# Sixteen of 32 experts ranked by token count on the chip, the last eight in blocks of four

## The chip, the cores and the metric

One core of one Trainium2 chip runs the whole kernel. The metric is the device time of one execution in microseconds (us), from its start to its end; the profile's span is the stretch from the first to the last instruction in it.

## The reference, cut to what matters

One layer of a decoder on 288 new tokens (256 of a prompt, 32 of eight samples), D = 2048, all weights float32: a mixer (convolution beside a gated recurrence, between the projections `w_in` and `w_out`), and then a mixture of 32 experts in 4 groups of 8. Each token takes the best group and in it the two best experts.

```python
def _hier_moe(h, w_rg, b_rg, w_re, b_re, w_gate, w_up, w_down):
    x = h.reshape(B * T, D)
    gprob = jax.nn.softmax((x @ w_rg + b_rg).astype(jnp.float32), axis=-1)
    p_top, g_idx = lax.top_k(gprob, 1)
    elog = (x @ w_re + b_re).astype(jnp.float32).reshape(-1, N_GROUPS, EXPERTS_PER_GROUP)
    elog_sel = jnp.take_along_axis(elog, g_idx[:, :, None], axis=1)[:, 0]
    e_val, e_idx = lax.top_k(elog_sel, TOP_K_IN_GROUP)
    e_w = jax.nn.softmax(e_val, axis=-1) * p_top
    ids = g_idx * EXPERTS_PER_GROUP + e_idx
    combine = jnp.sum(jax.nn.one_hot(ids, N_EXPERTS, dtype=jnp.float32) * e_w[..., None], axis=1)
    hid = jax.nn.silu(jnp.einsum('nd,edf->nef', x, w_gate)) * jnp.einsum('nd,edf->nef', x, w_up)
    hid = hid * combine[..., None].astype(hid.dtype)
    y = jnp.einsum('nef,efd->nd', hid, w_down)
    return y.reshape(B, T, D)
```

`w_gate` and `w_up` are 32 x 2048 x 512, `w_down` is 32 x 512 x 2048: 402.7 MB, which have to be read whatever the routing says. With the inputs of the test the experts 0 to 15 have 43, 35, 10, 39, 42, 6, 41, 36, 9, 28, 8, 14, 4, 22, 9 and 8 tokens, the experts 16 to 31 have 11, 17, 16, 17, 7, 36, 17, 7, 14, 21, 6, 8, 8, 26, 10 and 1.

## The kernel before

The stages follow each other in time: the projections of `w_in` with the mixer (to 450 us), 16 columns of `w_out` (to 577 us; `project`, split into a high and a low part), the routing (to 600 us), the experts (to 1592 us) and the final norm.

The experts go in 16 pairs. A `Pair` has 128 slots, 64 for each of its two experts (`CAP`), and tokens are put into slots by one-hot matmuls: `gather(q)` brings a quarter of the normalised tokens `h2` into `xg`, through the one-hot `P`; `gu(vi, q)` multiplies the slots with a quarter of the gate (vi = 0) or up (vi = 1) weights, the first expert in TensorE's columns 0 to 63 and the second in 64 to 127, so that both run side by side; `hidden` is silu times up, `turn` transposes it, `down(h, g)` multiplies with `w_down`, `out` weights the result, `combine` brings it back to the tokens through `PT`. A step, one (vi, q) or one (h, g), needs one load of 1 MiB (1.0486 MB) for each expert: 12 steps and 24 loads a pair, 384 loads in all. `mm` chains all these matmuls, so that TensorE runs them in the order in which they are written. The next pair's gathers stand between the steps of the pair before (`regular_pairs`).

All loads go through one DMA queue, SP's, in the order of use, into a ring of 14 slots: `xa` (3), `xb` (4), `raw` (3), `hi`, `lo` (2 each); a load waits until TensorE has read what its slot held. Four loads are issued during `w_out` (`load_ahead` at c = 3 to 6).

```python
        w = xslot(not isinstance(e, int)).rearrange("p (k c) -> p k c", c=1024 if which == 2 else 512)
        src = view[e, i] if isinstance(e, int) else view[bass.ds(e, 1), i].rearrange("e p k c -> (e p) k c")
        nc.sync.dma_start(out=w, in_=src)
```

Fifteen pairs run in a row; then 7 loads of the sixteenth are issued (`LASTPRE`), and all engines come to a branch: were there experts with over 64 tokens, pairs for these would run here (`overflow`; with these inputs none does). Then `last_pair` runs alone, with its gathers between its own gate steps.

The routing ends in `key`, the slot number of each token's two choices; it takes the place within an expert (`pr`, a triangular matmul over `mb`), the counts (`pn`) and what an overflow would add. The one-hot of pair 0 is made from `key`. ScalarE makes `h2` for the gathers (six activations), and the recurrence's states of heads 4 to 7 of the samples (`late_state`, eight units of two matmuls with a copy each) fill TensorE meanwhile.

Of the kernel before, what the change touches and what calls it, by code (L numbers as in the profile page):

```python
# [29 lines left out]
XPAIRS = 4  # L30
# [6 lines left out]
XA, XB = 3, 4  # L37
PRE = 3
LASTPRE = 7
# [16 lines left out]
def constants():  # L56
    p = np.arange(128)
    bq = np.zeros((8, 8, 4))
    for b in range(8):
# [15 lines left out]
        "full": np.broadcast_to((np.arange(NE) + 1) * float(CAP), (128, NE)),  # L75
        "xbase": np.broadcast_to(EXB - CAP - np.arange(NE) * float(CAP), (128, NE)),
# [28 lines left out]
def trunk_step(ctx: ExitStack, tc: tile.TileContext, a, o):  # L105
# [22 lines left out]
    rbias = const.tile([TT, 36], F32, name="rbias")  # L128
    lbc = const.tile([128, 8], F32, name="lbc")
# [216 lines left out]
    def router_rows():  # L346
# [6 lines left out]
        V.tensor_mul(wr3, wr3, nffn[:, :, None].to_broadcast([128, KT, 36]))  # L353
        nc.sync.dma_start(out=o["new_conv_sample"][0, :, 0:26].rearrange("b w c -> b (w c)"),
# [129 lines left out]
    def gate(j):  # L484
        finish(f"a{j - GB}")
# [327 lines left out]
    cr = sm.tile(list(CONSTS["cr"].shape), F32, name="cr")  # L813
    nc.sync.dma_start(out=cr, in_=a["cr"])
    onb = sm.tile([TT, TT], BF16, name="onb")
    V.memset(onb, 1.0)
    trib = sm.tile([TT, TT], BF16, name="trib")
    e64 = sm.tile([TT, NE], BF16, name="e64")
# [22 lines left out]
    def wlast(e0, e1, q, cuts):  # L841

        ws = [xslot().rearrange("p (k c) -> p k c", c=512) for _ in range(2)]
        for i in range(cuts):
            ks = slice(i * 4 // cuts, (i + 1) * 4 // cuts)
            for w, e in zip(ws, (e0, e1)):
                nc.sync.dma_start(out=w[:, ks], in_=wlv[e, q, :, ks])
        return ws

    def wload(which, e, q):  # L850
        if isinstance(e, int) and (which, e, q) in ahead:
            return ahead.pop((which, e, q))
        view = (wgv, wuv, wdv[:, q // 2])[which]
        i = q % 2 if which == 2 else q
        w = xslot(not isinstance(e, int)).rearrange("p (k c) -> p k c", c=1024 if which == 2 else 512)
# [22 lines left out]
    def late_state():  # L878
        for hh in range(4):
            st = ls0[hh // 2][:, hh % 2]  # L880
            for u in range(2):
                su = st[:, 4 * u:4 * u + 4]
                pn = bank("z")
                T.matmul(pn, lkm[:, hh], lvx[:, 4 * u:4 * u + 4], start=True, stop=False)
                T.matmul(pn, ident, su, start=False, stop=True)
# [5 lines left out]
    def load_ahead(i, e=0):  # L891
        which, q, u = i // 8, i % 8 // 2, i % 2
        ahead[which, e + u, q] = wload(which, e + u, q)

    for c in range(KT):
# [19 lines left out]
        if c == 6:  # L915
            V.tensor_copy(trib, C("tri")[:TT])
            V.tensor_copy(e64, C("e64")[:TT])
        if PRE <= c < PRE + XA + XB - 3:
            with tc.issue_after(loads[-1]):
                load_ahead(c - PRE)  # L920

# [28 lines left out]
    for t in range(NT):  # L950
        for u in range(2):
            us = slice(u * 1024, u * 1024 + 1024)
# [38 lines left out]
    oh = tv([TT, 2, NT, NE], "oh")  # L991
    for i in range(2):
        V.tensor_scalar(pk[:, i], od, float(i), None, op0=ALU.is_equal)
        V.tensor_mul(oh[:, i].rearrange("p t (g e) -> p t g e", e=8), b4(pk[:, i, :, None, :]),
                     b4(ohg[:, :, :, None]))

    pn, pr = bank("tp"), bank("o")
    for u in range(NT):
        T.matmul(pn[:TT, :NE], onb, mb[:, u], start=u == 0, stop=u == NT - 1)
# [6 lines left out]
    exn = tv([TT, NE, 4], "exn")  # L1006
    V.tensor_tensor(exn, pn[:TT, :NE, None].to_broadcast([TT, NE, 4]),
                    C("thr")[:TT, None, :].to_broadcast([TT, NE, 4]), op=ALU.is_gt)
    ex = sv([TT, 2, NE], "ex")
    V.reduce_sum(ex[:, 0], exn, axis=AX.X)  # L1010
    xs1 = sv([TT, NE + 1], "xs1")
    V.memset(xs1[:, 0:1], 0.0)
    V.tensor_tensor_scan(xs1[:, 1:], C("ones")[:TT], ex[:, 0], 0.0, op0=ALU.mult, op1=ALU.add)
    V.scalar_tensor_tensor(ex[:, 1], xs1[:, :NE], float(CAP), C("xbase")[:TT], op0=ALU.mult, op1=ALU.add)

    place = pr[:TT, 0:96].rearrange("p (t e) -> p t e", e=NE)
    kk = tv([TT, 2, NT, NE], "kk")
    key = sv([TT, 2, NT], "key")
    ov = tv([TT, NT, NE], "ov")
    V.tensor_tensor(ov, place, C("full")[:TT, None, :].to_broadcast([TT, NT, NE]), op=ALU.is_ge)  # L1020
    for i in range(2):
        V.tensor_mul(kk[:, i], oh[:, i], place)
    V.reduce_sum(key, kk, axis=AX.X)
    V.tensor_mul(oh, oh, ov[:, None].to_broadcast([TT, 2, NT, NE]))
    V.tensor_mul(oh.rearrange("p i t e -> p (i t) e"), oh.rearrange("p i t e -> p (i t) e"),
                 ex[:, None, 1].to_broadcast([TT, 2 * NT, NE]))
    kx = tv([TT, 2, NT], "kx")
    V.reduce_sum(kx, oh, axis=AX.X)
    V.tensor_add(key, key, kx)

    rows = sv([128, 4, N], "rows")
    xei = sv([1, 9], "xei", I32)
# [27 lines left out]
    def overflow_ids():  # L1060

        xid = sv([1, 8, NE], "xid")
        V.tensor_tensor(xid, xs1[0:1, None, 1:].to_broadcast([1, 8, NE]),
                        C("iota")[0:1, 0:8, None].to_broadcast([1, 8, NE]), op=ALU.is_le)
        xe = sv([1, 9], "xe")
        V.reduce_sum(xe[:, 0:8], xid, axis=AX.X)
        V.tensor_scalar(xe[:, 0:8], xe[:, 0:8], float(NE - 1), None, op0=ALU.min)
        V.tensor_copy(xe[:, 8:9], xs1[0:1, NE:NE + 1])
        V.tensor_copy(xei, xe)

# [22 lines left out]
    class Pair:  # L1093
        def __init__(self, e0, e1, base, last=False):
            self.e, self.base, self.last = (e0, e1), base, last
            self.pg, self.y = [], {}

        def onehot(self):
            kd = key
            self.P = P = X([TT, NT, 128], "P")  # L1100
            if self.base:
                kd = X([TT, 2, NT], "kd")
                V.tensor_scalar(kd, key, -float(self.base), None, op0=ALU.add)
# [53 lines left out]
        def down(self, h, g):  # L1157
# [3 lines left out]
            ws = [wload(2, e, 2 * h + g) for e in self.e]  # L1161
            for k in range(2):
                f = 2 * g + k
                for c in range(2):
                    for u, w in enumerate(ws):
                        mm(self.py[c][64 * u:64 * u + 64], self.hd[:, f, 64 * u:64 * u + 64],
# [49 lines left out]
    def regular_pairs():  # L1216

        ps = [Pair(2 * i, 2 * i + 1, 128 * i) for i in range(NE // 2 - 1)]
        before, py = None, None
        for n, p in enumerate(ps):  # L1220
            after = ps[n + 1] if n + 1 < len(ps) else None
# [172 lines left out]
```

## Time and profile before

| | us |
|---|---|
| median of 3 runs (1616.8 to 1619.52) | 1619.11 |
| the profiled execution | 1617.82 |
| its span | 1616.0 |
| TensorE busy | 1537.7 |
| VectorE busy | 676.2 |
| ScalarE busy | 455.9 |
| GpSimd busy | 31.8 |

The profiled execution lies 1.8 us over its span and 1.3 us under the median. The engines' busy times overlap. PE is TensorE, DVE is VectorE, ACT is ScalarE, SP issues the loads. A matmul of float32 stands as two instructions in the trace, so a step of a pair (8 matmuls) as x16.

### The profile page before, as it was taken

What the parts mean: (1) busy time and instruction counts of PE and PEld (TensorE: products, weight loads), DVE (VectorE), ACT (ScalarE), POOL (GpSimd) and SP (SyncE); (2) the same over time, 40 slices, a digit from 0 to 9 for tenths busy, and PEclk for the clock granted to TensorE, in tenths of its full rate; (3) what the DMA queues carried; (4) which work ended last, traced back from release to release, by engine and by line L of the source; (5) the groups of instructions that cost most, each with busy time, mean ns of one, the idle gap of its engine ahead of it and who ended that gap; (6) DMA issues with size and microseconds to landing.
All of it is one profiled execution on the core that took longest, in us unless ns stands there. A gap on an engine that the chain in (4) does not pass through costs nothing. (4 is left out here: it accounts for less than half of the span.)

```text
span 1616.0 us, 22366 instructions
## 1 busy us (share of the span) xinstructions
PE 1537.7 (95%) x9146; PEld 967.0 (60%) x9146; DVE 676.2 (42%) x1368; ACT 455.9 (28%) x980; POOL 31.8 (2%) x53
## 2 busy tenths in 40 slices
PE   5999999999979979999999999999999999999895
PEld 3999999999879944553553553453454454453431
DVE  4567787986554441312312412412412412312304
ACT  4477775976834450000000000000000000000003
POOL 1000001000000000000000000000000000000000
PEclk9999999999989989999999999999999999999897
DMA  8645456545496449999999999999999999999872
GB/s 210 174 121 144 136 157 195 150 127 142 112 290 166 154 175 343 401 415 410 423 411 415 419 417 402 425 416 412 422 414 416 422 414 414 421 419 410 360 266 59
DMA packets 228309, 492.78 MB, mean 305 GB/s; under 512 B 13593, under 2 KB 157545, under 8 KB 194936
## 3 DMA queue, kind: packets, MB, share of 16 engines
q1 hardware_dynamic: 225448, 485.09, 80.2%
q0 software_dynamic: 2608, 6.13, 1.1%
q8 instruction: 74, 1.21, 0.3%
q14 instruction: 35, 0.29, 0.0%
q10 hardware_dynamic: 144, 0.07, 0.0%
HBM read 483.92 MB, written 8.18 MB: 305 GB/s over the span
## 5 line engine op out<-in xcount | busy, mean ns | idle before, releaser
L1086 PEld LDWEIGHTS tp<-P,h 96*128 96x128 f32 x1536 | 177.8, 194 | 41.5 <-issue 22.0
L1086 PE MATMUL att<-xb,xg 128*64 128x512 f32 x584 | 199.2, 598 | 0.8 <-DVE xg L1117 0.8
L1086 PE MATMUL tp<-P,h 96*128 96x128 f32 x1536 | 187.3, 281 | 9.7 <-DVE xg L1117 4.8
L195 DVE TENSOR_TENSOR lo<-raw,hi 128x1024 fp32r<-128x1024 f32 x124 | 147.7, 1221 | 50.5 <-ACT hi L194 50.3
L194 ACT CAST hi<-raw 128x1024 fp32r<-128x1024 f32 x124 | 123.8, 1049 | 82.5 <-PE z L199 60.6
L1086 PE MATMUL att<-lo,xg 128*64 128x512 f32 x296 | 133.8, 602 | 0.8 <-issue 0.8
L1086 PE MATMUL att<-xa,xg 128*64 128x512 f32 x448 | 132.3, 595 | 1.6 <-DVE xg L1117 1.6
L1171 ACT ACTIVATE yh<-o,wc 128x512 fp32r<-128x512 f32 x64 | 44.0, 687 | 313.5 <-PE o L1086 281.8
L1147 DVE TENSOR_TENSOR hid<-hid,att 128x512 f32<-128x512 f32 x16 | 11.0, 688 | 285.5 <-PE att L1086 285.5
L1086 PE MATMUL att<-raw,xg 128*64 128x512 f32 x432 | 128.4, 595 | 1.6 <-DVE xg L1117 1.6
L1086 PE MATMUL att<-hi,xg 128*64 128x512 f32 x288 | 128.2, 594 | 0.0
L1182 DVE TENSOR_TENSOR acc<-acc,z 96x512 f32<-96x512 f32 x120 | 76.9, 680 | 116.8 <-PE z L1086 116.6
L198 PE MATMUL z<-hhb,hi 128*128 128x288 f32 x368 | 112.1, 305 | 0.0
L200 PE MATMUL z<-hhb,lo 128*128 128x288 f32 x368 | 110.9, 301 | 0.0
L199 PE MATMUL z<-hla,hi 128*128 128x288 f32 x368 | 110.9, 301 | 0.0
L199 PE MATMUL z<-hlb,hi 128*128 128x288 f32 x368 | 110.6, 301 | 0.0
L1117 DVE TENSOR_TENSOR xg<-tp,npm 128x512 f32<-128x512 f32 x64 | 44.3, 692 | 158.0 <-PE tp L1086 157.9
L198 PE MATMUL z<-hha,hi 128*128 128x288 f32 x368 | 110.2, 299 | 0.0
L200 PE MATMUL z<-hha,lo 128*128 128x288 f32 x368 | 109.8, 298 | 0.0
L1172 DVE SCALAR_TENSOR_TENSOR yl<-o,wc,yh 128x512 fp32r<-128x512 f32 x64 | 47.9, 748 | 140.6 <-ACT yh L1171 138.6
L1155 ACT COPY hd<-tp 128x512 f32<-128x512 f32 x16 | 9.4, 586 | 295.3 <-PE tp L1086 295.3
L1146 ACT ACTIVATE hid<-att 128x512 f32<-128x512 f32 x16 | 9.6, 597 | 290.8 <-PE att L1086 248.5
(417 smaller groups left out, 2779.8 us busy)
## 6 DMA issues: line engine op xcount, KB each, us to landing
raw<-in_w_in_dram SPq DMA_DIRECT2D x48, 1024.0 KB, 5.9
xb<-in_w_exp_gate_dram SPq DMA_DIRECT2D x37, 1024.0 KB, 18.6
xb<-in_w_exp_up_dram SPq DMA_DIRECT2D x36, 1024.0 KB, 12.5
xb<-in_w_exp_down_dram SPq DMA_DIRECT2D x35, 1024.0 KB, 13.5
xa<-in_w_exp_gate_dram SPq DMA_DIRECT2D x30, 1024.0 KB, 17.6
raw<-in_w_exp_gate_dram SPq DMA_DIRECT2D x27, 1024.0 KB, 17.4
xa<-in_w_exp_down_dram SPq DMA_DIRECT2D x27, 1024.0 KB, 13.1
raw<-in_w_exp_down_dram SPq DMA_DIRECT2D x27, 1024.0 KB, 13.4
```

The lines of the kernel that those rows point to most:

```text
L194: S.copy(wh[:, ks], w[:, ks])
L195: V.tensor_sub(wl[:, ks], w[:, ks], wh[:, ks].bitcast(F32))
L198: T.matmul(ps[:, :N], wh[:, k], xh[k], start=i == 0, stop=False)
L199: T.matmul(ps[:, :N], wh[:, k], xl[k], start=False, stop=False)
L200: T.matmul(ps[:, :N], wl[:, k], xh[k], start=False, stop=i == KT - 1)
L1086: i = f(*args, **kw)
L1117: V.tensor_mul(self.xg[:, 4 * q:4 * q + 4], pb, npm[:, 4 * q:4 * q + 4, None].to_broadcast([128, 4, 128]))
L1146: si = S.activation(self.hid, self.pg[0], AF.Silu)
L1147: V.tensor_mul(self.hid, self.hid, self.pg[1])
L1171: S.activation(yh, py, AF.Copy, scale=self.wc[:, 2:3])
L1172: V.scalar_tensor_tensor(yl, py, self.wc[:, 2:3], yh.bitcast(F32), op0=ALU.mult, op1=ALU.subtract)
L1182: V.tensor_add(av, av, ps[t][:TT])
```

## The change

Experts 0 to 15 stay in 8 pairs of 64 slots each. Experts 16 to 31 are ranked on the chip by their token count (`keys`, `ids`; the ranks' expert numbers go to `eid`). Ranks 0 to 7 form four pairs of 64 slots, ranks 8 to 15 two blocks of four experts with 32 slots each; `Block` takes the place of `Pair` and gives `128 // len(e)` slots to an expert. The order is: eight pairs, the first block of four, ten loads of the second (`MIDPRE`), the branch, the second block of four, the four ranked pairs, the last of them with the end (`last_down`). A block of four has the same 12 steps as a pair, with four loads in each. The expert numbers of the ranked blocks come from registers, so that their loads (192 of 384) have addresses that are worked out at run time.

The ring gets 16 slots (`XA` 4, `XB` 5), and six loads are issued during `w_out`. The constants `cr` are loaded at the start of the kernel. `h2` is scaled in another order, first halves first. The first one-hot comes from a short key (`key01`, of `pr` and `mb` alone, since the first pair is always experts 0 and 1). Two heads of `late_state` come ahead of the routing, and the other two behind the first gate step in TensorE's fixed order. `last_down` puts its matmuls in the written order too.

```diff
+NST = 16
+NDP = 4
+NQ = 2
-XA, XB = 3, 4
+XA, XB = 4, 5
-LASTPRE = 7
+MIDPRE = 10
...
+        nc.sync.dma_start(out=cr, in_=a["cr"])
...
-    for t in range(NT):
-        for u in range(2):
-            us = slice(u * 1024, u * 1024 + 1024)
+    for u in range(2):
+        us = slice(u * 1024, u * 1024 + 1024)
+        for t in range(NT):
             S.activation(by_four(h2[t][:, us], 0), by_four(acc[:, t, us], 1), AF.Copy, scale=rs2[:, t:t + 1])
...
+    key01 = sv([TT, NT, 2], "key01")
+    V.tensor_add(key01, nm, place[:, :, 0:2])
...
+        V.scalar_tensor_tensor(nj, cnt[:, NST:], float(NE), iot[:, :m], op0=ALU.mult, op1=ALU.subtract)
+        gt = e2[:, 96:96 + m * m].rearrange("p (e f) -> p e f", f=m)
+        V.tensor_tensor(gt, nj[:, None, :].to_broadcast([TT, m, m]), nj[:, :, None].to_broadcast([TT, m, m]),
+                        op=ALU.is_gt)
+        V.reduce_sum(rk, gt, axis=AX.X)
...
+    class Block:
+
+        def __init__(self, es, base, over=False):
+            self.e, self.base, self.over = tuple(es), base, over
+            self.w = 128 // len(self.e)
...
+        def rows(self, u):
+            return slice(self.w * u, self.w * (u + 1))
...
-            ws = [wload(vi, e, q) for e in self.e]
+            ws = [wload(vi, e, q, self.over) for e in self.e]
             for i in range(4):
                 k = 4 * q + i
                 for u, w in enumerate(ws):
-                    mi = mm(self.pg[vi][64 * u:64 * u + 64], self.xg[:, k, 64 * u:64 * u + 64], w[:, i],
+                    mi = mm(self.pg[vi][self.rows(u)], self.xg[:, k, self.rows(u)], w[:, i],
                             start=k == 0, stop=k == KT - 1)
...
-                        if q == 0:
-                            late_state()
+                        if first and q == 0:
+                            late_state((2, 3), mm)
                         if q < 3:
                             p.gather(q + 1)
-                        if q == 0:
+                        if first and q == 0:
                             with tc.issue_after(pi.ins), tc.issue_after(mi.ins):
+                                k = keys()
                                 weights()
-                                overflow_ids()
+                                ids(*k)
...
-                    T.matmul(py[64 * u:64 * u + 64], p.hd[:, f, 64 * u:64 * u + 64], w[:, f], start=f == 0, stop=f == 3)
+                    mm(py[p.rows(u)], p.hd[:, f, p.rows(u)], w[:, f], start=f == 0, stop=f == 3)
...
+    def static_id(j):
+        return nc.values_load(eid[0:1, j:j + 1], engines=[mybir.EngineType.SP], min_val=NST, max_val=NE - 1,
+                              skip_runtime_bounds_check_because="ranks are a permutation of the later experts")
...
+    def quad(i):
+        return Block([static_id(2 * NDP + 4 * i + u) for u in range(4)], b0 + 128 * i)
...
+    in_a_row(blocks + [Later(lambda: quad(0))], first=True)
+    q1 = quad(1)
...
+    for i in range(MIDPRE):
+        load_ahead(i, q1.e)
     regular = nslot[0]
...
-    last_pair(Pair(NE - 2, NE - 1, 128 * (NE // 2 - 1), last=True))
+    in_a_row([q1] + [Later(lambda i=i: Block([static_id(2 * i + u) for u in range(2)], NST * CAP + 128 * i))
+                     for i in range(NDP)], last=True)
```

On TensorE, at the first gate step of the program, before (`h_6200` to `h_6202` are the `h2` of the three token tiles, `z<-xb` the units of `late_state`, `att<-xa` the gate step):

```order
L1086 MATMUL tp<-P,h_6201 128x128
L1086 MATMUL tp<-P,h_6202 128x128
L884 MATMUL z<-xb 128x512
L885 MATMUL z<-xb,ident 128x512
L1086 MATMUL att<-xa,xg 64x512 x8
L1086 MATMUL tp<-P,h_6200 128x128
L1086 MATMUL tp<-P,h_6201 128x128
```

The same place now (`h_6222` to `h_6224`):

```order
L1062 MATMUL tp<-P,h_6224 128x128
L1062 MATMUL att<-xa,xg 64x512 x8
L1062 MATMUL z<-xb 128x512
L1062 MATMUL z<-xb,ident 128x512
L1062 MATMUL z<-xb 128x512
L1062 MATMUL z<-xb,ident 128x512
L1062 MATMUL z<-xb 128x512
L1062 MATMUL z<-xb,ident 128x512
L1062 MATMUL z<-xb 128x512
L1062 MATMUL z<-xb,ident 128x512
L1062 MATMUL tp<-P,h_6222 128x128
```

One unit of `late_state` stood ahead of the first gate step, and two more ahead of the first gather; now four stand between the first gate step and the second gather, and none ahead of the step.

On VectorE, now, from the short key to the start of the long one (`key_6270` is `key01`; the tiles with a k ahead are those of `keys`):

```order
L1014 TENSOR_TENSOR key_6270<-nm,o 96x6
L1162 TENSOR_TENSOR P<-cr,key_6270 96x384
L1075 COPY khd<-o 96x96
L1077 COPY kPT<-tp 96x32
L1081 TENSOR_SCALAR pk<-od 96x24 x2
```

The end of that stretch, 42 rows behind `P` (`xg` is the product of the first gather, that the first gate step reads; `pt<-ge` stands 14 rows behind `P`, and `ge` comes from ScalarE, behind the six activations of `h2`):

```order
L1123 TENSOR_REDUCE kpj<-khid 96x6
L1040 TENSOR_TENSOR wts<-wts,dd 96x3
L1115 TENSOR_TENSOR kPT<-kPT,cr 96x32
L1113 SCALAR_TENSOR_TENSOR kpj<-cr,kPT 96x32
L1180 TENSOR_TENSOR xg<-tp,npm 128x512
```

Before, `xg` of the first gather stood behind the end of the key, the one-hots of two pairs and the weights; now behind most of `keys`, `weights` and `ids`.

On SP's queue, now, loads of the second block of four, ahead of the branch (`eid` holds the expert numbers, an ISA row works out an address):

```order
L1397 TENSOR_LOAD eid
L867 ISA
L867 DMA xa<-in_w_exp_gate_dram 128x2048
L867 ISA
L867 DMA xb<-in_w_exp_gate_dram 128x2048
L867 ISA
L867 DMA xb<-in_w_exp_gate_dram 128x2048
L867 ISA
L867 DMA lo<-in_w_exp_gate_dram 128x2048
```

The same queue before, in a stretch of the loads of the pairs:

```order
L857 DMA xa<-in_w_exp_gate_dram 128x2048 x2
L857 DMA xa<-in_w_exp_up_dram 128x2048
L857 DMA xb<-in_w_exp_up_dram 128x2048
L857 DMA raw<-in_w_exp_up_dram 128x2048 x3
L857 DMA hi<-in_w_exp_up_dram 128x2048
L857 DMA lo<-in_w_exp_up_dram 128x2048
```

Each load of a ranked expert has an ISA row of its own ahead of it, and each of the 16 ranked experts a TENSOR_LOAD; the loads of experts 0 to 15 have neither.

## Rows read from the trace of the kernel before

**Rows 1.** the page: busy time, share of the span and instructions of TensorE

```profile
PE 1537.7 (95%) x9146; PEld 967.0 (60%) x9146; DVE 676.2 (42%) x1368; ACT 455.9 (28%) x980; POOL 31.8 (2%) x53
```

**Rows 2.** timeline of ScalarE: the silu of pairs one and fifteen (start, duration)

```profile
631.20 0.60 ACT L1146 ACTIVATE hid<-att 128x512 f32<-128x512 f32 x1 [12.12 <-PE att L1086]
...
1478.19 0.60 ACT L1146 ACTIVATE hid<-att 128x512 f32<-128x512 f32 x1 [16.88 <-PE att L1086]
```

**Rows 3.** windows: busy time and count by engine, granted clock, DMA share, GB/s

```profile
586.00:596.00 10.00, 2.69 (x13) 1.65 (x13) 7.15 (x40) 8.77 (x7) 0.90 (x1) 0.50 0.00 2
...
700.00:1000.00 300.00, 298.27 (x1572) 139.92 (x1570) 86.87 (x180) 19.66 (x30) 0.00 (x0) 1.00 1.01 416
```

**Rows 4.** waits of the SP queue from 500 us: total, times, longest

```profile
SPq L857 <- PE att L1086: 364.2, 119, 8.8
...
SPq L857 <- PE o L1086: 310.8, 58, 12.0
```

**Rows 5.** windows, as above: inside the steady state, and around the branch

```profile
1020.00:1030.00 10.00, 10.00 (x58) 4.96 (x56) 3.73 (x10) 1.37 (x2) 0.00 (x0) 1.00 1.01 424
...
1508.00:1512.00 4.00, 4.00 (x20) 1.54 (x16) 1.49 (x4) 0.69 (x1) 0.00 (x0) 1.00 1.02 428
...
1512.00:1516.00 4.00, 3.23 (x14) 1.62 (x12) 4.00 (x8) 0.69 (x1) 0.00 (x0) 1.00 0.90 375
...
1516.00:1520.00 4.00, 0.30 (x2) 0.00 (x0) 2.10 (x8) 0.00 (x0) 0.00 (x0) 1.00 0.38 156
...
1520.00:1524.00 4.00, 2.89 (x14) 2.92 (x15) 2.89 (x12) 0.00 (x0) 0.00 (x0) 0.65 0.31 78
```

**Rows 6.** timeline of TensorE in the second pair: one step

```profile
714.57 3.65 PE L1086 MATMUL o<-xb,hd 128*64 128x512 f32 x16
```

**Rows 7.** timeline of TensorE: eight matmuls with 32 columns each

```profile
399.34 0.69 PE L450 MATMUL tp<-sqc,on 128*32 128x288 f32 x8
...
399.96 0.40 PE L198 MATMUL z<-hhb,hi 128*128 128x288 f32 x1
```

**Rows 8.** timelines of ScalarE and VectorE in the routing

```profile
581.50 12.21 ACT L953 ACTIVATE h<-acc,rs 96x1024 f32<-96x1024 f32 x6 [0.61 <-DVE rs L172]
...
594.80 0.16 DVE L1044 TENSOR_REDUCE pt<-ge 96x3 f32<-96x12 f32 x1 [2.25 <-ACT ge L1038]
```

**Rows 9.** timeline of TensorE at the first gather

```profile
600.42 2.84 PE L1086 MATMUL tp<-P,h 96*128 96x128 f32 x24
...
603.10 1.02 PE L884 MATMUL z<-xb 128*128 128x512 f32 x2
...
604.91 3.65 PE L1086 MATMUL att<-xa,xg 128*64 128x512 f32 x16
...
608.50 0.71 PE L1086 MATMUL tp<-P,h 96*128 96x128 f32 x4
```

**Rows 10.** timelines of the SP queue, and of TensorE behind the branch

```profile
1510.69 0.33 SPq L857 DMA_DIRECT2D lo<-in_w_exp_up_dram  x1
...
1521.74 1.28 SPq L857 DMA_DIRECT2D raw<-in_w_exp_up_dram  x3
...
1521.11 5.38 PE L1086 MATMUL tp<-P,h 96*128 96x128 f32 x24 [4.82 <-DVE P L1106]
```

**Rows 11.** timelines at the end, and two groups of the page

```profile
1570.92 3.65 PE L1276 MATMUL o<-xb,hd 128*64 128x512 f32 x16 [0.73 <-ACT hd L1155]
...
1598.30 0.40 PE L1282 MATMUL att<-yl,PT 128*96 128x512 f32 x1
...
1601.45 0.68 DVE L1284 TENSOR_TENSOR acc<-acc,att 96x512 f32<-96x512 f32 x1
...
L1171 ACT ACTIVATE yh<-o,wc 128x512 fp32r<-128x512 f32 x64 | 44.0, 687 | 313.5 <-PE o L1086 281.8
...
L1172 DVE SCALAR_TENSOR_TENSOR yl<-o,wc,yh 128x512 fp32r<-128x512 f32 x64 | 47.9, 748 | 140.6 <-ACT yh L1171 138.6
```

More of the change, by code (lines that the diff above doesn't have):

```diff
@@ L876, in late_loads, with late_state @@
                      C("hm2")[:, :, None].to_broadcast([128, 4, 128]))
-    def late_state():
-        for hh in range(4):
+    def late_state(heads, mul):
+        for hh in heads:
             st = ls0[hh // 2][:, hh % 2]
@@ L920, in trunk_step @@
                 load_ahead(c - PRE)
+    late_state((0, 1), T.matmul)
     def sv(shape, name, dt=F32):
@@ L990, in trunk_step @@
     V.tensor_mul(mb.rearrange("p t (g e) -> p t g e", e=8), b4(pk[:, 2, :, None, :]), b4(ohg[:, :, :, None]))
[L991 to L999, printed above, removed]
+    nm = tv([TT, NT, 2], "nm")
+    V.tensor_scalar(nm, mb[:, :, 0:2], -float(EXB), float(EXB), op0=ALU.mult, op1=ALU.add)
+    pr, pn = bank("o"), bank("tp")
     for t in range(NT):
@@ L1004, in trunk_step @@
         T.matmul(pr[:TT, t * NE:(t + 1) * NE], trib, mb[:, t], start=False, stop=True)
[L1006 to L1014, printed above, removed]
+    for u in range(NT):
+        T.matmul(pn[:TT, :NE], onb, mb[:, u], start=u == 0, stop=u == NT - 1)
     place = pr[:TT, 0:96].rearrange("p (t e) -> p t e", e=NE)
-    kk = tv([TT, 2, NT, NE], "kk")
+    key01 = sv([TT, NT, 2], "key01")
+    V.tensor_add(key01, nm, place[:, :, 0:2])
     key = sv([TT, 2, NT], "key")
[L1019 to L1029, printed above, removed]
     rows = sv([128, 4, N], "rows")
-    xei = sv([1, 9], "xei", I32)
+    xei = sv([1, 2 * XPAIRS + 1], "xei", I32)
+    eid = sv([1, NE - NST], "eid", I32)
     def weights():
@@ L1214, in pair_alone, with in_a_row @@
             p.combine(c, CT)
-    def regular_pairs():
-        ps = [Pair(2 * i, 2 * i + 1, 128 * i) for i in range(NE // 2 - 1)]
-        before, py = None, None
+    def in_a_row(ps, first=False, last=False):
+        prev, py = None, None
         for n, p in enumerate(ps):
-            after = ps[n + 1] if n + 1 < len(ps) else None
+            end = last and n == len(ps) - 1
+            nxt = ps[n + 1] if n + 1 < len(ps) else None
             if n == 0:
@@ L1235, in regular_pairs @@
                                 weights()
-                                overflow_ids()
-                    if before is not None and vi == 0 and q < 2:
-                        before.out(2 + q, py[q])
-                        before.combine(2 + q, CT)
+                                ids(*k)
+                    if prev is not None and vi == 0 and q < 2:
+                        prev.out(2 + q, py[q])
+                        prev.combine(2 + q, CT)
                 if vi == 0:
-                    if after is not None:
-                        after.onehot()
+                    if nxt is not None:
+                        nxt.onehot()
@@ L1243, in regular_pairs @@
+                    if end:
+                        final_weights()
                     p.slots()
-            p.hidden()
-            if after is not None:
-                after.gather(0)
-                after.gather(1)
+            si = p.hidden()
+            if end:
+                last_down(p, si)
+                return
+            if nxt is not None:
+                nxt.gather(0)
+                nxt.gather(1)
             p.turn()
-            if after is not None:
-                after.gather(2)
@@ L1251, in regular_pairs @@
-            py = pair_down(p, (lambda: after.gather(3)) if after is not None else lambda: None)
-            before = p
+            if nxt is not None:
+                nxt.gather(2)
+            py = pair_down(p, (lambda: nxt.gather(3)) if nxt is not None else lambda: None)
+            prev = p
         for c in (2, 3):
-            before.out(c, py[c - 2])
-            before.combine(c, CT)
-    def last_pair(p):
-        p.onehot()
-        p.gather(0)
-        for vi in range(2):
-            for q in range(4):
-                p.gu(vi, q)
-                if vi == 0 and q < 3:
-                    p.gather(q + 1)
-        final_weights()
-        p.slots()
-        si = p.hidden()
+            prev.out(c, py[c - 2])
@@ L1281, in last_pair @@
                 for i, y in enumerate((yh, yl)):
[L1282 removed]
+                    mm(pz[:TT], p.PT[:, t * TT:(t + 1) * TT], y, start=i == 0, stop=i == 1)
                 av = acc[:, t, c * 512:(c + 1) * 512]
@@ L1341, in trunk_step @@
     regular = nslot[0]
-    nx = nc.values_load(xei[0:1, 8:9], min_val=0, max_val=8,
-                        skip_runtime_bounds_check_because="a sum of at most eight overflow tiles")
+    nx = nc.values_load(xei[0:1, 2 * XPAIRS:2 * XPAIRS + 1], min_val=0, max_val=2 * XPAIRS,
+                        skip_runtime_bounds_check_because="a sum of at most nine overflow tiles")
     def overflow(i):
         with tc.If(nx > 2 * i):
-            ids = [nc.values_load(xei[0:1, 2 * i + u:2 * i + u + 1], engines=[mybir.EngineType.SP],
-                                  min_val=0, max_val=NE - 1,
-                                  skip_runtime_bounds_check_because="clamped to the last expert on the chip")
-                   for u in range(2)]
+            xs = [nc.values_load(xei[0:1, 2 * i + u:2 * i + u + 1], engines=[mybir.EngineType.SP],
+                                 min_val=0, max_val=NE - 1,
+                                 skip_runtime_bounds_check_because="clamped to the last expert on the chip")
+                  for u in range(2)]
```

165 lines of the change are left out of this document (117 added, 48 removed).

## The prediction

> **What bounds the kernel now.** I read the page first, then the windows of the expert stage, the silu of each pair, and last the waits of the load queue. TensorE is busy for 1537.7 of the 1616.0 us of the span [rows 1]. In the expert stage it is busy for 298.27 of 300 us at the full clock (granted 1.00, that is 2.4 GHz), while the DMA engines move 416 GB/s with a share of 1.01 [rows 3]. Both look full, so neither row alone tells which one sets the pace. The silu does: the fifteenth stands 1478.19 - 631.20 = 846.99 us behind the first, that is 14 intervals of 60.50 us [rows 2]. A pair's 24 loads of 1.0486 MB in 60.50 us are 416 GB/s, just what the window shows. Who waits for whom is in the queue's own waits: from 500 us on SP waited 364.2 us in 119 places for a gate or up matmul and 310.8 us in 58 for a down matmul, each time for the slot that the matmul read [rows 4]. So the loads wait for TensorE: **the expert stage is bound by TensorE**, with the stream of loads close behind. How close: where slots are at hand the stream shows 424 GB/s in ten microseconds and 428 in four [rows 5]. I take 425, that is 2.467 us a load and 59.2 us a pair. Making TensorE faster by a half would therefore give 2% of the stage and no more; what counts is how far the loads can follow.
>
> **Blocks of four: TensorE.** A step of a pair is 16 instructions in some 3.5 us (3.65 with the last one's tail) [rows 6]: the two experts' columns run side by side. That four column tiles also run together is seen in another stage: eight matmuls with 32 columns each and 288 moving columns are all begun and done in 0.62 us (399.34 to 399.96) [rows 7], where in the step 16 with 512 moving columns take 3.5 us, two by two. By columns, two at a time would want 8/16 x 288/512 x 3.5 = 0.98 us for these eight, four at a time 0.49; the row is nearer to four. So a step of four experts costs TensorE some 3.5 us as a pair's does, and a block of four about 60.5 us, as a pair. Two blocks of four in the place of four pairs take 2 x 60.5 = 121 us of work from TensorE.
>
> **Blocks of four: the stream.** The 384 loads stay. A step of a block of four needs four loads, 9.87 us of the stream; a block needs 48, 118.4 us. There TensorE waits, and the stream sets the pace; in the pairs TensorE sets it again (60.5 against 59.2). So the gain is not 121 us, it is what the loads are ahead: the 1.3 us a pair by which the stream is quicker, and the slots filled when the first block of four begins.
>
> **The front.** The diff makes the way to the first gather shorter, but the order on VectorE puts the product `xg` of that gather behind 42 rows of the long key, and the fourteenth of these, `pt<-ge`, hangs on ScalarE's `ge`, that stands behind six activations of `h2`. Those end at 593.7 and let `pt` start at 594.80 after 2.25 us of waiting [rows 8]; that stays. 28 rows of some 0.2 us follow (`pt` itself took 0.16), so `xg` starts at about 601. The first gate step started at 604.91 before [rows 9], and will at about 601.5. TensorE will have idled since its first gather, and its granted clock was 0.50 (1.2 GHz) in the idle stretch from 586 to 596 [rows 3]; a step that takes 3.6 us at the full clock loses some 3 us at the start. Then four units of `late_state` follow in fixed order, of which one took 604.91 - 603.10 = 1.8 us [rows 9]: 7.2. The second gather starts at 601.5 + 3.6 + 3 + 7.2 = 615.3, before at 608.50 [rows 9]. For the earlier constants `cr` at the start of `w_out` I take 1 us off (0 to 4; nothing shows it directly). The first silu comes at about 631.2 + 6.8 - 1, say **636.6** (632 to 641), so the front loses 5 us.
>
> **The sum.** Seven more static pairs: silu of the eighth at 636.6 + 7 x 60.5 = 1060.1. From a silu to the next pair's first gate step are four up steps and the rest of the pair, 14.0 + 29.4 us (60.5 less 17.1 for four gate steps with two combines between them). The first block of four starts at 1103.5. Of the ring's 16 slots two are then being read and one is in flight: 13 loads of the blocks of four lie there. TensorE waits for the last time at the last up step of the first ranked pair, whose 16th load it needs. Up to it 96 + 16 - 13 = 99 loads have to come, 99 x 2.467 = 244.2 us, and the branch stops the stream once. Before, its windows lost (428 - 375) + (428 - 156) + (428 - 78) GB/s in 4 us each, 2.7 MB or 6.3 us [rows 5], with a next load 11 us behind the last one ahead [rows 10]. Now ten loads lie ahead of it and not seven, and the stop is in the midst of the run; between nothing and 6.3 I take 3.3. That gives 1103.5 + 247.5 = 1351. Then 3.5 for that step, 29.4 for the rest of the pair, 17.1 for the next gate: silu of the second ranked pair at 1401. Two more pairs: 1522.
>
> The end: four up steps 14.0, silu, transposes and `hd` 2.2. Then four times a down step 3.58, the weighting, and a combine. Before, TensorE needed 1570.92 to 1598.70 with adds behind it to 1602.1 [rows 11], since the scheduler put the next down step into the wait. Now the order is as written: TensorE waits each time for 0.69 us on ScalarE and 0.75 on VectorE [rows 11], with hand-overs 1.7, and six combine matmuls take 1.45. 4 x (3.58 + 1.7 + 1.45) = 26.9, but VectorE has no backlog at the end. Last matmul at 1565. From the last add's start to the end of the span are 1616.0 - 1601.45 = 14.6 us [rows 11], which stay: 1580. The profiled execution lies 1.8 over its span, so **1582** (the median shown is another 1.3 higher than that execution; that is in the range).
>
> **Prices that hide.** SP issues a load in 0.33 us, or three in 1.28 [rows 10]; 192 loads now have an address from registers. No row shows such a load. They may cost up to 2.467 us each with nothing lost, since the stream takes that for each. The 42 rows of ranking are in the front already. Weights of the end's norm in the last block, and the six loads ahead during `w_out`, lie beside TensorE's work.
>
> **Where the notes speak against it.** In the last pair before, TensorE idled some 5 us up to 1521.11, and the granted clock was 0.65 in the window behind that; 24 gather instructions took 5.38 us there [rows 10] where they took 2.84 at the full clock [rows 9]. In a block of four TensorE waits 9.87 - 3.5 = 6.4 us in each gate or up step. The Trainium skill, TensorE: Matmul & The Clock Gate, HAM oscillation, says that short bursts with DMA waits between them send the clock back to the lower level at every burst; the rows at the branch agree. At the lower level a step takes 7.1 us, still less than 9.87, so by rule or not the gate and up halves stay with the stream. The skill's page DMA: Bandwidth & Descriptors, Specifications, puts one core's HBM limit at about 358 GB/s; by that 99 loads would take 290 us, not 244, and the time would be 1628. 416 GB/s over 300 us [rows 3] say that it does not hold here.
>
> **Rivals.**
> 1. *The clock stays low in the second half of a block of four too* (downs, gathers, combines). For it: the idle stretches above. Against it: in that half TensorE's work lies closer together, gathers fill the waits. Price: the rest of the second block of four takes 58.8 in the place of 29.4 us behind its loads, and a gate step more: 1582 + 29.4 + 3.5 = 1615, no change. Half of it: 1598. Chance 0.04 for the whole, 0.12 for a part (1587 to 1600).
> 2. *Four tiles run only two by two* with 512 moving columns, 7.1 us a step. Four down steps of the last block lose up to 14 us together, as far as loads don't hide them: 1582 to 1596, middle 1589. Chance 0.05.
> 3. *The stream cannot do more than 416*: 2.521 us a load, 99 x 0.054 = 5.3 more: 1587. Chance 0.12; for it, it is the long run's figure; against it, it is TensorE's pace.
> 4. *The front gets shorter, as the diff's order of the key has it* (`xg` served early in fact, at 594, full clock): silu 8 us sooner, 1574. Chance 0.08.
> 5. *The other side: SP cannot keep up.* Its place is the 192 loads with addresses from registers. At x us each they cost 192 x (x - 2.467); from x = 2.65 on all 36 us are gone, at 3 the time is 1582 + 102 = 1684. For it: each has an instruction of its own ahead of the DMA; against it: 0.33 to 0.43 us for an issue [rows 10]. Chance 0.04.
>
> The forecast itself (1574 to 1590) keeps 0.55. Range 1567 to 1604: it leaves out rival 5, the whole of rival 1, and the edges of 2 and 4. 0.2% (3.2 us) is about what a measurement of this kernel can tell from no change. Faster 0.91, the same 0.04, slower 0.05.
>
> **What the profile after would show.** Silu intervals of 60.5 us for the first eight blocks, near 118 us in the blocks of four, 60.5 again behind them. In the blocks of four SP waits for no slot, GB/s near 425, TensorE half idle, its waits on DMA; a granted clock under 1.00 there, and step durations that tell rivals 1 and 2 apart (starts of four matmuls within 0.03 us, or two). First silu at 632 to 641, `xg` near 601. GB/s under 400 in the blocks of four with SP busy issuing would mean rival 5. The prediction is wrong if the blocks of four take over 125 us each, or if the ranked pairs behind them go on waiting for loads.

## The result and the profile after

The changed kernel takes 1597.94 us (median of 4 runs, 1596.67 to 1599.1), the kernel before 1619.07: a ratio of 0.9872, interval 0.9855 to 0.9889, 21 us faster. Forecast were 1582 and a range of 1567 to 1604. The profiled execution has a span of 1596.6 us, where the sum had 1580.

A line of the page, to compare with [rows 1]:

```profile
PE 1468.3 (92%) x8898; PEld 918.8 (58%) x8898; DVE 644.8 (40%) x1317; ACT 448.2 (28%) x968; POOL 31.9 (2%) x53
```

The silu of some blocks, timeline of ScalarE: the first pair, the two blocks of four, the first, second and fourth ranked pair (as [rows 2]):

```profile
634.09 0.60 ACT L1209 ACTIVATE hid<-att 128x512 f32<-128x512 f32 x1 [12.12 <-PE att L1062]
...
1118.05 0.60 ACT L1209 ACTIVATE hid<-att 128x512 f32<-128x512 f32 x1 [16.91 <-PE att L1062]
...
1247.41 0.60 ACT L1209 ACTIVATE hid<-att 128x512 f32<-128x512 f32 x1 [47.80 <-PE att L1062]
...
1342.49 0.60 ACT L1209 ACTIVATE hid<-att 128x512 f32<-128x512 f32 x1 [17.86 <-PE att L1062]
...
1409.20 0.60 ACT L1209 ACTIVATE hid<-att 128x512 f32<-128x512 f32 x1 [16.88 <-PE att L1062]
...
1530.87 0.60 ACT L1209 ACTIVATE hid<-att 128x512 f32<-128x512 f32 x1 [16.88 <-PE att L1062]
```

The first pairs keep their 60.5 us. From the first to the second block of four 129.4 us pass (branch included), then 95.1 and 66.7, and 60.8 on average behind that. Windows of the same kernel, columns as [rows 3]:

```profile
1101.00:1203.00 102.00, 75.53 (x424) 20.43 (x416) 15.08 (x25) 4.07 (x7) 0.00 (x0) 0.90 1.02 415
1203.00:1224.00 21.00, 10.27 (x49) 6.61 (x52) 8.57 (x36) 0.00 (x0) 0.00 (x0) 0.59 0.76 303
1224.00:1350.00 126.00, 105.94 (x652) 43.27 (x646) 20.82 (x45) 4.53 (x7) 0.00 (x0) 0.95 1.02 416
...
1120.00:1130.00 10.00, 5.75 (x33) 1.32 (x34) 0.00 (x0) 0.00 (x0) 0.00 (x0) 1.00 1.02 423
1160.00:1170.00 10.00, 5.90 (x36) 1.25 (x32) 0.00 (x0) 0.00 (x0) 0.00 (x0) 1.00 1.03 406
1290.00:1300.00 10.00, 7.96 (x64) 2.40 (x66) 0.69 (x1) 0.00 (x0) 0.00 (x0) 1.00 1.02 399
```

In the blocks of four TensorE waits and the stream runs all the time, at 415 to 416 GB/s, but for the branch. The short windows say what that mean is made of: 423 in an up half (the stretch of the four up steps), 406 and 399 in a down half (the four down steps). The up and gate loads bring rows of 8 KB, the down loads rows of 4 KB. And so the prediction's last wait, timeline of TensorE in the up half of the first ranked pair:

```profile
1358.71 3.65 PE L1062 MATMUL att<-hi,xg 128*64 128x512 f32 x14 [1.32 <-DMA hi<-in_w_exp_up_dram]
```

It is the step that was forecast, with the wait for a load that was forecast, 10 us later than its place: 1358.7, where the sum had 1351 less 2.5 for the earlier front.

### The profile page after: what moved, and what is told of

Its sections match the earlier page's. It is cut to its first block, busy times and chain, and to the rows that moved or that the text cites. A ratio compares the mean times of both kernels' runs of the same rounds, so it can differ in the third digit from the quotient of the medians.

```text
span 1596.6 us, 22199 instructions
## 1 busy us (share of the span) xinstructions
PE 1468.3 (92%) x8898; PEld 918.8 (58%) x8898; DVE 644.8 (40%) x1317; ACT 448.2 (28%) x968; POOL 31.9 (2%) x53
## 5 line engine op out<-in xcount | busy, mean ns | idle before, releaser
L1062 PE MATMUL att<-xb,xg 128*64 128x512 f32 (+1 forms) x640 | 175.2, 634 | 11.9 <-DMA xb<-in_w_exp_up_dram 9.6
L1062 PEld LDWEIGHTS tp<-P,h 96*128 96x128 f32 x1344 | 158.3, 196 | 42.8 <-issue 24.0
L1062 PE MATMUL tp<-P,h 96*128 96x128 f32 x1344 | 166.9, 283 | 15.1 <-DVE P L1169 8.6
L1062 PE MATMUL att<-raw,xg 128*64 128x512 f32 (+1 forms) x384 | 119.8, 617 | 8.5 <-DMA raw<-in_w_exp_up_dram 7.0
L1062 PE MATMUL att<-xa,xg 128*64 128x512 f32 (+1 forms) x512 | 106.9, 618 | 10.2 <-DVE xg L1180 6.6
L1245 DVE TENSOR_TENSOR acc<-acc,z 96x512 f32<-96x512 f32 x104 | 66.6, 680 | 118.2 <-PE z L1062 118.0
L1062 PE MATMUL att<-lo,xg 128*64 128x512 f32 (+1 forms) x256 | 101.2, 620 | 2.9 <-DMA lo<-in_w_exp_up_dram 2.9
L1235 DVE SCALAR_TENSOR_TENSOR yl<-o,wc,yh 128x512 fp32r<-128x512 f32 x56 | 41.9, 748 | 150.3 <-ACT yh L1234 148.7
L1062 PEld LDWEIGHTS att<-xb,xg 128*64 128x64 f32 (+1 forms) x640 | 49.1, 136 | 91.0 <-issue 69.8
L1062 PE MATMUL att<-hi,xg 128*64 128x512 f32 (+1 forms) x256 | 89.8, 597 | 5.7 <-DMA hi<-in_w_exp_up_dram 5.7
```

Of the source, the lines that this page charges most:

```text
L1062: i = f(*args, **kw)
L1235: V.scalar_tensor_tensor(yl, py, self.wc[:, 2:3], yh.bitcast(F32), op0=ALU.mult, op1=ALU.subtract)
L1245: V.tensor_add(av, av, ps[t][:TT])
```

## The experiments

My theory: the loads set the pace from the first block of four to that last up step, at 16 loads of 8 KB rows with 421 GB/s and 8 of 4 KB rows with 406 in 24, and the branch stops them once. The rivals: TensorE itself (32-column tiles, its clock), the branch's wait on TensorE, or the end. Each ratio is against runs of the kernel before on the same chip, whose medians were 1619.5, 1617.9 and 1618.9. The diffs are cut to the lines that matter.

**Half the loads.** In `gu`, and likewise in `down` and for the loads ahead of the branch:

```diff
-            ws = [wload(vi, e, q, self.over) for e in self.e]
+            ws = [wload(vi, e, q, self.over) for e in self.e[:2]] * (len(self.e) // 2)
```

> In the blocks of four the third and fourth expert use the weights of the first and second: the same matmuls, half the loads (48 fewer); the output is not the reference's. Theory (TensorE needs 60.5 us for a block of four, all above is waiting for loads): the blocks of four take some 61 us each, with the branch between them, and the time is 1505 to 1520. Rival (the blocks of four are slow on TensorE itself, by 32-column tiles that don't run together or by the lower clock): over 1570.

Measured: 1507.0 (one execution), span 1505.3. Windows between the silus of the two blocks of four and of the first ranked pair (1119.1, 1197.3, 1257.7):

```profile
1119.00:1180.00 61.00, 50.49 (x380) 21.32 (x372) 18.85 (x51) 3.93 (x6) 0.00 (x0) 0.89 0.90 366
1180.00:1240.00 60.00, 58.09 (x505) 29.03 (x496) 12.41 (x27) 3.25 (x5) 0.00 (x0) 1.00 0.95 360
```

A block of four now takes 60.4 us, as a pair does, and 78.2 where the branch lies between. In its second window TensorE is busy for 58.09 of 60 us at the full clock and the stream has room (360 GB/s), so that this is TensorE's own time. The 48 loads are worth 91 us: so much of the changed kernel's time in the blocks of four is waiting for loads. And the tiles of 32 columns run four together: four matmuls, one for each expert, start within 0.02 us (1186.69 to 1186.71 in this run's timeline of TensorE).

**Gate and up matmuls twice.** In `gu`, for four experts:

```diff
+                n = 2 if len(ws) == 4 else 1
+                for r in range(n):
-                for u, w in enumerate(ws):
+                    for u, w in enumerate(ws):
```

> Every gate and up matmul of the two blocks of four is done twice into the same sum; the output is not the reference's. TensorE's work there grows by 2 x 8 x 3.5 = 56 us. Theory (TensorE waits for loads there, and its clock costs nothing): the time moves by less than 3 us, 1596 to 1601, and the granted clock in these halves is nearer to 1.00. Rival (TensorE or its clock sets the pace in a part of them): 1605 or more; or, if the lower clock cost time, 1590 to 1595.

Measured: 1598.8 (1594.9 to 1601.3). The same stretches as above:

```profile
1101.00:1203.00 102.00, 91.11 (x680) 27.02 (x678) 15.02 (x25) 4.62 (x7) 0.00 (x0) 0.95 1.01 409
1224.00:1350.00 126.00, 118.28 (x910) 49.15 (x902) 20.82 (x45) 4.53 (x7) 0.00 (x0) 0.99 1.02 416
```

Twice the gate and up matmuls make 28 us more of busy TensorE (56 were expected; why not more was not looked into), the clock is nearer to full, and the time is the same. Neither TensorE's work in these halves nor its lower clock costs anything.

**All pairs.** `quad(i)` gives two experts, with the slots to suit:

```diff
-        return Block([static_id(2 * NDP + 4 * i + u) for u in range(4)], b0 + 128 * i)
+        return Block([static_id(2 * NDP + 2 * i + u) for u in range(2)], b0 + 128 * i)
```

> The two blocks of four are four pairs of 64 slots again, still ranked and with addresses from registers; all else is as in the changed kernel (ring of 16, branch amid the pairs, front, end). Theory (the blocks of four alone bring the gain; the rest loses some 3 us at the front and 7.6 by the norm's weights and wins a little at the branch): 1617 to 1625. Rival (the ring, the branch and the end bring it, since the stream is as slow with pairs): 1598 to 1605.

Measured: 1627.3 (one execution), span 1625.5, 2 us over the range of the theory. Of the 9.5 us over the span of before, 5.0 are at the front (first silu 636.2), 3.2 at the branch (an interval of 80.0 and not 76.8), 1.3 behind the last silu. So the blocks of four by themselves are worth some 29 us, and the rest of the change costs some 8.

**Rows of 8 KB, for measuring.** In `wload` the down loads take gate weights:

```diff
-        view = (wgv, wuv, wdv[:, q // 2])[which]
+        view = (wgv, wuv, wgv)[which]
```

> The loads of the down weights read gate weights in their place, in rows of 8 KB and not of 4 KB; the last block's down loads stay; the output is not the reference's. Theory (the stream sets the pace from the first block of four to the first ranked pair, and the down loads are its slow part, 406 GB/s against 421): the windows of the down halves in the blocks of four show 420 or more, 32 down loads of that stretch take 2.49 us each and not 2.59, the last up step of the first ranked pair comes 3 to 4 us sooner, and the time is 1594 to 1595. Rival (406 comes from TensorE's slots in the down half, not from the rows): windows and time as before the edit, 1598.

Measured: 1592.8 (ratio 0.9832, 0.9816 to 0.9849). The down windows of above:

```profile
1160.00:1170.00 10.00, 5.72 (x32) 1.29 (x32) 0.00 (x0) 0.00 (x0) 0.00 (x0) 1.00 1.01 421
1290.00:1300.00 10.00, 7.58 (x46) 1.79 (x42) 0.00 (x0) 0.00 (x0) 0.00 (x0) 0.84 1.02 424
```

The dips are gone, and 5 us with them; the last up step of the first ranked pair starts at 1356.1, 2.7 us sooner, though in this execution the first silu came 1.2 us later than in the changed kernel's. The rows were it. (Here the same gate weights are read twice; the last experiment has real down weights in rows of 8 KB.)

**The product of the first gather ahead of the long key.** `gather` hands back its product `gi`:

```diff
-                            with tc.issue_after(pi.ins), tc.issue_after(mi.ins):
-                                k = keys()
+                            with tc.issue_after(gi.ins), tc.issue_after(mi.ins):
+                                k = keys(*kt)
```

> The long key's work on VectorE comes behind the product of the first gather (two copies out of PSUM stay ahead of it). Theory (the first gate step waits 6.6 us for that product): it starts at about 593.5 and not at 599.4, the first silu comes at 628 to 630 and not at 634.1, and all of it is there at the end: 1592 to 1594. Rival (the stream of loads, not TensorE, is late, so that an earlier start only waits later): silu sooner, time 1597 to 1598.

Measured: 1591.7 (ratio 0.9832, 0.9816 to 0.9848), 6 us less. The first gate step of the changed kernel and, below, of this one:

```profile
599.40 5.19 PE L1062 MATMUL att<-xa,xg 128*64 128x512 f32 x16 [6.60 <-DVE xg L1180]
```

```profile
593.42 3.65 PE L1062 MATMUL att<-xa,xg 128*64 128x512 f32 x16 [0.78 <-DVE xg L1184]
```

The wait is gone, and the step runs at the full clock. The first silu is at 626.6, 7.5 sooner, and 7 us of the span are won: TensorE gives slots back sooner, so the stream is sooner too. By 1350 it has brought 294.7 MiB since 577 us, 2.7 more than in the changed kernel, and these are 6.8 us of the stream at 416 GB/s.

**The norm's weights by DMA, alone and with the product first.** In `final_weights`, for the eight matmuls with one row:

```diff
+        G.dma_start(out=fin["nf"], in_=a["norm_final"][None, :].to_broadcast([TT, D]))
```

> The final norm's weights are spread over the partitions by a DMA and not by eight matmuls with one row. Theory (these matmuls cost 5.0 us on TensorE and some 2.6 us of lower clock behind them): silu of the last block to the end takes 58 us and not 65.7, the granted clock stays at 1.00 in its up half, time 1590 to 1591. Rival (the end waits for the last loads anyway): the up half gets shorter, but a down step of the end waits for a load, time 1594 to 1598.

> Both edits together: the norm's weights by DMA, and the product of the first gather ahead of the long key. Theory: the two add, 7.6 and 5 us less, 1584 to 1587. Rival (the stream of loads bounds one of them): 1588 to 1592.

Measured: 1596.8 and 1591.3. The first is within the interval of the changed kernel's time, the second within that of the product alone. The theory fell. Timeline of TensorE in the last block's up half, of the changed kernel and of the one with the DMA alone:

```profile
1537.59 1.95 PE L1357 MATMUL z<-nfr,one 1*96 1x512 f32 x4
...
1540.48 3.04 PE L1357 MATMUL z<-nfr,one 1*96 1x512 f32 x4
...
1543.44 5.48 PE L1062 MATMUL att<-xb,xg 128*64 128x512 f32 x13
```

```profile
1543.22 3.22 PE L1062 MATMUL att<-xb,xg 128*64 128x512 f32 x13 [1.34 <-DMA xb<-in_w_exp_up_dram]
```

And the latter's window in which the norm's DMA runs:

```profile
1510.00:1520.00 10.00, 10.00 (x44) 3.67 (x43) 5.17 (x8) 1.37 (x2) 0.00 (x0) 1.00 1.01 335
```

The eight matmuls took 5.0 us and left a slow step behind them. Without them the step waits for its loads, and while the norm's own DMA runs (0.8 MB for 96 partitions) the engines are as busy (share 1.01) but move only 335 GB/s. The loads bound the last block too. The two profiles differ by more than that, though: from the last silu to the end it takes 61.8 us now and not 65.7, but the last silu comes 3.0 us later, and the silu of the second ranked pair is 3.2 later already (1412.4), which lies ahead of all that was edited. So how much of the 3.9 us the loads take back is not shown by this pair of runs alone.

**Without the branch.** `overflow(0)` and its register are left out:

```diff
-    overflow(0)
```

> The branch with the blocks for experts with too many tokens is left out (with these inputs it is not taken). Theory (it stops the stream for 5.7 us, and the stream sets the pace there): no window of the second block of four under 400 GB/s, time 1591 to 1593. Rival (TensorE's 8.6 us wait at the branch is what counts): 1588 to 1590. Rival (hidden): 1598.

Measured: 1603.6 (ratio 0.9908, 0.9892 to 0.9925): 6 us slower, which none of the three had. No window of ten microseconds between 1200 and 1270 is under 419 GB/s, so the stop was gone, and by 1350 just as many bytes had come as in the changed kernel (291.8 MiB from 577 us on, against 292.0). Yet the last up step of the first ranked pair starts at 1365.8, 7 us later. The marks that a load leaves on its semaphore show how. There are 16 for each load, one from each DMA engine; the Trainium skill, DMA: Bandwidth & Descriptors, Why a DMA increments its semaphore by 16 and not by 1, says that the engines finish independently and that only the last mark means a landed load. The traces agree: the load that this step needs has its first mark at 1354.7 and its last at 1365.8, when the step starts; in the changed kernel they stand at 1356.4 and 1358.7. Mean time from a load's first to its last mark, for loads that landed in 50 us from each start:

```
from us             650    900   1050   1150   1250   1300   1350   1450
before              2.7    5.1    7.1    6.4    7.2    6.7    6.3    6.9
changed             2.6    4.4    4.1    5.9    2.0    2.2    2.3    3.4
without branch      2.2    6.3    8.8   10.7   10.8   11.4   10.8   10.4
with a stop, below  2.5    7.6    9.5   10.8    1.6    4.7    7.1    8.7
matmuls twice       2.3    3.1    3.3    3.0    2.0    2.6    2.9    4.2
8 KB, above         1.7    2.1    3.4    2.9    2.0    2.7    2.7    3.7
whole rows, below   1.9    1.5    1.7    2.3    1.9    1.9    2.2    3.5
```

The engines drift apart, and a stop of the stream (the branch, near 1215) puts them together. A load that is spread over 11 us is late though its bytes are not. But the kernel without the branch is wider apart at 1050 us already (8.8 against 4.1), where the branch has no part yet, and so is the next one (9.5). Why is open, and with it how much of the 6 us comes from the missing stop.

**A stop in the branch's place.** To the kernel without the branch, behind the tenth load ahead, the eleventh being held back until it:

```diff
+    held[:] = [nc.sync.dma_start(out=scr, in_=w[0:1, 0, 0:8]).ins]
```

> The kernel without the branch, which took 1603.6, and in the branch's place one small copy on the load queue that reads the tenth load ahead, with the eleventh load behind it: the queue waits there until the tenth has landed on all 16 DMA engines. Theory (without the branch the engines drift apart, a load's first and last mark lie some 9 to 11 us apart from 1000 us on, and a matmul waits for the last one; a stop of the stream puts them together again): the spread falls to 2 to 3 us behind the copy, and the time is 1593 to 1600, though the copy itself stops the stream for 2 to 5 us. Rival (the spread is a mark of something else, such as slow rows of 4 KB): 1604 to 1608.

Measured: 1611.6, slower by 8 and outside the ranges of both. The spread did fall, to 1.6 us. But the copy waited for the whole spread stream to come in, from 1208.7 to 1228.1, and by 1350 the kernel had 287.3 MiB, 4.5 less, which at 416 GB/s (2.52 us a MiB) is 11.3 us. Its last up step of the first ranked pair starts at 1373.3, only 7.5 later than without the stop (1365.8). So some 4 us came back; the load of that step has its marks 7.1 us apart and not 11.1, which is just these 4. That the spread costs time is borne out by both runs; as a cure the stop is too dear.

**The end in the scheduler's order.**

```diff
-                    mm(py[p.rows(u)], p.hd[:, f, p.rows(u)], w[:, f], start=f == 0, stop=f == 3)
+                    T.matmul(py[p.rows(u)], p.hd[:, f, p.rows(u)], w[:, f], start=f == 0, stop=f == 3)
```

> The down and combine matmuls of the last block are left to the scheduler's order again, as in the kernel before. From the first down step to the end of the span the kernel before took 1616.0 - 1570.9 = 45.1 us and the changed one 1596.6 - 1555.0 = 41.6. Theory (the written order costs TensorE waits but takes the backlog off VectorE): 3 to 4 us more, 1600 to 1602. Rival (the order in the end is hidden by the last loads): 1598. Rival (the waits between the steps cost more than the backlog): 1592 to 1595.

Measured: 1599.1 (ratio 0.9886, 0.987 to 0.9903), not to be told from the changed kernel. From the last silu to the end it takes 63.3 us and not 65.7, but the last silu comes 2.7 us later; what the order in the end is worth is not seen in the time.

**Whole rows in earnest.** A down load takes 128 rows of 8 KB, with four sums at a time, the combines behind the next block's gate steps, and the product of the first gather first:

```diff
-            if g == 0:
-                self.py = [bank("o") for _ in range(2)]
+            if f == 0:
+                self.py = [bank(t) for t in ("att", "att", "o", "o")]
```

> The down loads take 128 whole rows of 8 KB (and not 256 half rows of 4 KB), with four sums at a time in the banks of the gate and up sums and of the down sums; the combines go behind the four gate steps of the next block; and the product of the first gather comes ahead of the long key. Theory (5 us for the rows, 6 for the product, and they add): 1586 to 1589. Rival (TensorE now waits for a bank at the start of each block, 1 to 1.5 us in 12 pairs): intervals of 61.5 or more, 1597 to 1606. Rival (they don't add): 1590 to 1592.

> As the kernel with rows of 8 KB and the product first, and the final norm's weights by DMA. Theory (with a quicker stream TensorE is the bound in the last block, so the 5 to 7 us of the eight matmuls come off): 1579 to 1584. Rival (that DMA's 0.8 MB goes into the stream just ahead of the last loads, and the last block waits for them): 1586 to 1589, no gain over the kernel without it.

Measured: **1579.5** (ratio 0.976, 0.9744 to 0.9776), and with the norm's weights by DMA 1579.1 (0.9754, 0.9737 to 0.977). The first is 6.5 us below its theory's range. Pairs keep 60.5 us, so no bank is waited for. Windows in a down half of the first block of four, and in the ranked pairs:

```profile
1160.00:1170.00 10.00, 5.72 (x32) 1.28 (x32) 0.00 (x0) 0.00 (x0) 0.00 (x0) 1.00 1.02 423
...
1400.00:1450.00 50.00, 49.66 (x269) 24.92 (x266) 10.05 (x16) 3.33 (x5) 0.00 (x0) 1.00 1.01 421
```

That is 18 us faster than the changed kernel and 39 faster than the one before, and 5 to 7 more than the two parts had given singly (by the ratios or by the medians). By the profiles the first silu is 6.6 us sooner than in the changed kernel, the first interval 1.7 us shorter (58.8), the way from there to the silu of the second ranked pair 7.4 shorter, and the end 2.8. The smaller spread (1.5 to 2.3 us up to the blocks of four) and the combines in the gate steps, where TensorE waits in a block of four, can both have part in it; that was not taken apart. The norm's weights by DMA bring nothing here either: the end gets 1.0 us shorter (61.9 and not 62.9), and its time, though in the range that was expected, is that of the kernel without them.

## Why the prediction was right in direction and too good by 16 us

- **The mechanism held.** The blocks of four cost TensorE a pair's time each (60.4 us with half the loads), the loads set the pace in them, the last such wait of any size is at the last up step of the first ranked pair, and 99 loads up to it were right: 99.9 by the bytes between 1101 and 1358.7. Rival 1 (clock) and rival 2 (tiles) fell: the clock did fall, to 0.90 and 0.95 over the two stretches (1.00 in its three ten-microsecond windows above), and cost nothing. The prediction named over 125 us for a block of four as a sign of being wrong: the first took 129.4 with the branch, 123.7 less the 5.7 us that this cost.
- **The steps that failed are the stream's 425 and the end.** The 425 was read off the first two windows of [rows 5], and by the DMA records all that came in these was in rows of 8 KB. The mean with the down loads is 415.5, so 99.9 loads cost 252 us and not 246, 5.7 more. This is rival 3, with its price, for a reason that it didn't have: 416 is not TensorE's pace alone. 16 loads at 421 and 8 at 406 GB/s take 39.9 + 20.7 = 60.5 us, just what a pair takes on TensorE, which keeps its 60.5 when the rows are quicker. So by these rates both were the bound before, and 121 us less work on TensorE could give no more than the loads that lie ahead and the stops of the stream.
- **The branch** cost the stream (1 - 303/416) x 21 = 5.7 us where 3.3 was taken, 2.4 more; the load more than counted is another 2.2. Without the branch the time is not better but worse, with a spread of the loads that no term had.
- **The front** came at 634.1, forecast 636.6 (632 to 641; the prediction's own terms make 637.0): `xg` started at 598.7 (VectorE's timeline) and not 601, behind `ge` as was said. Part of these 2.5 us is chance: the other runs with the same front have their first silu at 634.3 to 636.2. What the front costs is found again at the end, as the product put first shows.
- **The end** took 65.7 us from the last silu, not 58: the largest term. I had put the norm's weights beside TensorE's work at no cost. They took 5.0 us and some 2.6 us of lower clock behind them, but without them the end still takes 61.8, since the loads are next, and the time is the same. The intervals of the ranked pairs gave 0.7 more (one up step, at 1419.3, took 4.29 us and not 3.60; what it waited for is not shown).
- Together: -2.5 + 5.7 + 2.4 + 2.2 + 7.7 + 0.7 = 16.2 of the 16.6 us. The time lies outside the forecast proper (1574 to 1590), and within the range only since that left room for rivals, of which rival 3 alone came, and that for a third of the miss.
- **SP kept up** with addresses from registers; rival 5 did not show: the stream ran at 415 and over there.

## What to carry to other kernels

Where two engines show full, work out both times from rows of their own: here the loads' 60.5 us by kind of row would have said that halving TensorE's work frees little beyond the loads that lie ahead. Read the rate of a stream by the shape of its transfers (here by row length), not by its best windows. A part that costs nothing while the pairs set the pace, such as a front that is late or a combine in the wrong half, is worth its full time once another thing is the bound: find out which waits come next before a part is called hidden.

## What was not expected of the hardware

- Rows of 4 KB move at 399 to 406 GB/s, of 8 KB at 421 to 424, in the same queue with 16 busy engines; by the DMA records of 640 to 1600 us a piece of 8 KB takes 312 ns in the median and one of 4 KB 160 (16 engines at these medians make 420 and 410 GB/s, an estimate). Some pieces of both kinds take over 700 ns, 72 of 8 KB and 20 of 4 KB in the changed kernel. The last block's down loads come in pieces of 2 KB, and at 387 GB/s (the last line below).
- The 16 DMA engines drift apart by up to some 11 us in a stream that isn't stopped, and a load counts when the last one is done. How fast they drift differs by kernel, on one chip as well (near 1150, twice: 3.0 us, without branch: 10.7); why is open. With rows of 8 KB it stayed under 4 us in each run, but it did so with rows of 4 KB too (twice), up to 4.2.
- Eight matmuls with one row in use, run among full ones, came with a granted clock of 0.50 from 1541.2 to 1548.0, though TensorE was busy all the time. It isn't so in every run: with all pairs the clock stayed at 1.00 behind the same eight, and with rows of 8 KB it was low for half as long.

```profile
1537.00:1544.00 7.00, 7.00 (x16) 1.72 (x14) 0.00 (x0) 2.19 (x4) 0.00 (x0) 0.80 1.03 390
1544.00:1548.00 4.00, 4.00 (x12) 1.18 (x10) 0.00 (x0) 0.13 (x1) 0.00 (x0) 0.50 1.05 387
```
